# Two query blocks moved from beside the scan into the opening of a hybrid decoder layer

## The chip, the cores and the metric

The kernel runs on one core of a Trainium2 chip. The metric is the device time of one execution, in microseconds (us), as the median of several runs. The engines are named as in the profile: PE (TensorE, matrix products; PEld is its weight load), DVE (VectorE), ACT (ScalarE), POOL (GpSimd) and SP (SyncE, which here only issues transfers). Each has its own queue and works through it in order; semaphores join them. PE writes its results to PSUM, eight banks of 512 f32 values a partition, from which DVE or ACT copies them out.

## What is computed

One layer of a decoder, for a prompt of 1024 tokens and 8 single sample tokens that share the weights (1032 columns of tokens in all). All of it is in f32. With `xn` the root-mean-square norm of `x`:

```
sc_b, sc_c, sc_x, z, xbc, dt_raw, q, gates = split(xn @ w_in)      # w_in: 1024 x 12320
y_a = (sc_b * conv3(sc_c * sc_x)) @ w_sc_out
xs, B, C = split(silu(conv4(xbc) + bias));  dt = softplus(dt_raw + dt_bias)
y_b = group_rmsnorm((ssd(xs, dt, a, B, C) + d * xs) * silu(z)) @ w_ssm_out
y_c = softmax(q . k_mem / 16) . v_mem @ w_attn_o                   # 4 heads of 256, 256 memory tokens
x  += (g_a * y_a + g_b * y_b + g_c * y_c) @ w_merge_o
x  += swiglu(rmsnorm(x));   y = rmsnorm(x)
```

`ssd` is a state-space scan over 8 chunks of 128 tokens, in 4 groups of 8 heads. The columns of `w_in` that matter here are `xbc` (24 blocks of 128 columns; block 16 is B of group 0, called B0, and block 20 is C of group 0, called C0), `dt_raw` (32 columns), and `q` (8 blocks of 128, two to a head).

## The kernel before

Every projection is computed in blocks of 128 output columns for all 1032 tokens. A weight block of 1024 x 128 is loaded raw (512 KB, `load_raw`, line 139, one of three buffers), then split into a rounded part `hi` (an ACT cast) and the rest `lo` (a DVE subtraction). The activations are split likewise into `ah` and `al`. A product is then three passes, hi x ah, hi x al and lo x ah, over 8 pieces of the 1024 inputs. In `gemm` (line 218) the 1032 tokens are taken as 260 + 512 + 260 columns, so a block is 8 x 3 x 3 = 72 matmuls into three PSUM banks.

The stages that matter here are these.

The opening makes xn. The tokens are taken in four quarters of 256 (the last has 264, with the sample tokens). For a quarter, `square` sums squares (ACT), `root_of` makes the inverse root on ACT and DVE, turns it by PE (`ps_rb`, line 516) and copies it to `rbc`. `tokens` then turns two of the eight 128-wide pieces at a time by PE (`ps_xt`), scales them on DVE (`xw`, line 522), casts on ACT (`xnh`, line 523), subtracts on DVE (`xnl`, line 524), and copies the turned x to a buffer `xt` and stores it. Beside this, `first_products` (lines 597 to 599) computes B0 and C0 for the quarter before, 3 matmuls of 256 columns for each piece and block, and `step_sizes` (line 607) computes `dt_raw` with 16 small matmuls a quarter. B0 and C0 have three PSUM banks each (`ps_b0`, `ps_c0`); two more are shared by all the turns (`sm_ps`). After the opening comes the turn of the step sizes (`ps_dtT`, line 692) and the first two blocks of z (`z_step`).

Then follow long stages for z, xbc, the gates and the short convolution, which the change doesn't touch.

The scan stage comes after the last gate pair. Its work is cut into small pieces, which stand in a queue `pend`. Matrix blocks, called fillers, run on PE in between: 8 query blocks (`q_step`, which projects one block, scales it on ACT, copies the sample columns to `qs` and stores the block to `q_d`), then blocks of the output projections (`out_part`, `wo0x`, `wo1x`, `wo2x`). `pace` says how many pieces are issued in each block: the length of `pend` over 18 blocks (8 fillers, 8 of the first output projection and 2 of the second). The attention then is cut up in the same way, beside the output blocks that are left, less 1.4 (14 - 1.4 = 12.6 blocks).

The order of instructions on each engine is set by a scheduler that works from the program's order and its own estimates, and not by the program text alone.

Of the kernel before, what the change touches and what calls it, by code (L numbers as in the profile page):

```python
# [43 lines left out]
def tile_kernel(ctx: ExitStack, tc, a, o):  # L44
# [3 lines left out]
    def f32(t):  # L48
        return t.bitcast(F32)
# [390 lines left out]
    with tc.tile_pool(name="p0", bufs=1) as p0, tc.tile_pool(name="pop", bufs=1, space=PSUM) as pop:  # L440
        ps_b0, ps_c0 = (
            [pop.tile([P, 512], F32, tag=f"{n}{i}", name=f"ps_{n}{i}") for i in range(3)] for n in ("B", "C")
        )
        xin = []
# [8 lines left out]
        for col, name in ((16 * P, "wB0"), (20 * P, "wC0")):  # L453
            loaded[name] = load_raw(wblock(w_in, C_XBC + col), name)
        w_dt = load_raw(wblock(w_in, C_DT), "wdt")
        for i in range(2, NCK):
            load_x(i)
        xs_sb = p0.tile([NS, D], F32, tag="xs", name="xs_sb")
        SY.dma_start(xs_sb, a["x_sample"][:, 0, :])

        PC["mix"] = 200
# [9 lines left out]
        for key, src, n in (  # L471
# [13 lines left out]
            while done < n:  # L485
                b, off = divmod(at, P)
                m = min(n - done, P - off)
                SY.dma_start(rows[off : off + m, b, :], r[done : done + m, :])
                done += m
                at += m  # L490
        def par(key, i):
            return prm[:, PC[key] + i : PC[key] + i + 1]
# [65 lines left out]
        def root_of(g):  # L558
# [3 lines left out]

            ps = sm_ps(f"ps_rb{g}") if g else ps_c0[2]
            turn(g, ps, 0, lambda i, t, n: bc(rst[:n, 2 * g + i : 2 * g + i + 1], [n, P]))
# [24 lines left out]

        def first_products(g, k):  # L590
            c, n = part(g), parts[g][1]
            ah, al = xn[k]
            ks = slice(k * P, (k + 1) * P)
            for ps, (wh, wl) in ((ps_b0, w_b0), (ps_c0, w_c0)):
                bank, at_c = places[g]
                po = ps[bank][:, at_c : at_c + n]
                PE.matmul(po, wh[:, ks], ah[:, c], start=(k == 0), stop=False)
                PE.matmul(po, wh[:, ks], al[:, c], start=False, stop=False)
                PE.matmul(po, wl[:, ks], ah[:, c], start=False, stop=(k == order[-1]))

        def step_sizes(g):
# [3 lines left out]
            for k in range(KD):  # L605
                q = k % 4
                PE.matmul(
                    ps[q * HEADS : (q + 1) * HEADS, :n], w_dt[:, k * P : k * P + HEADS], xw[k][:, c],
                    start=(k < 4), stop=(k >= 4),
# [8 lines left out]
        with tc.issue_after(mix_in):  # L618
            square(0, 1)
        ahead_ = [sm_ps(f"ps_xt0{i}") for i in range(2)] + [ps_b0[1], ps_c0[1]]  # L620
        for i, (t, n) in enumerate(srcs[0]):
# [4 lines left out]
        for g in range(4):  # L626
            steps_ = [order[2 * i : 2 * i + 2] for i in range(4)] if g < 3 else [(k,) for k in order]
            for i, ks in enumerate(steps_):
                last_x, scaled = tokens(g, ks)
                if g == 0 and i == 0:  # L630
                    w_b0, w_c0 = first_weights(scaled, last_x)
# [12 lines left out]
        firsts = [ev_tile("u" + n) for n in ("B0", "C0")]  # L644
        for u, ps in zip(firsts, (ps_b0, ps_c0)):
            S.copy(u[:, 3 : 3 + 512], ps[0])
            S.copy(u[:, 3 + 512 : 3 + 768], ps[1][:, :256])
        for k in order[:4]:
            first_products(3, k)
        step_sizes(3)  # L650
        for k in order[4:]:
            first_products(3, k)
        for u, ps in zip(firsts, (ps_b0, ps_c0)):
            S.copy(u[:, 3 + 768 : 3 + TT], ps[2][:, : TT - 768])

# [768 lines left out]
    def plain():  # L1424
        loaded["wq0"] = load_raw(wblock(w_in, C_Q), "wq0")
        load_group(0)
# [13 lines left out]
    fillers = deque()  # L1440
    for i in range(8):
        fillers.extend(q_step(i))
# [76 lines left out]
    for g in range(GROUPS):  # L1519
# [747 lines left out]
```

## Time and profile before

| | us |
|---|---|
| median of 3 runs | 2427.4 (2425.25 to 2427.65) |
| profiled execution | 2428.33 |
| its span | 2426.6 |
| PE busy in the span | 2397.0 |
| DVE busy | 1613.8 |
| ACT busy | 1091.9 |

The profile is one execution, recorded instruction by instruction. A row of the timeline has the start, the duration, the engine, the line of the kernel, the operation, and out<-in by the names of the tiles, with the shape and a count. Where the engine was idle before it, square brackets say how long, and whose result ended the wait. Successive matmuls overlap in the pipeline, so their durations add up to more than the time they take; the distance from start to start tells the pace. A row of a table of stretches has the stretch, its length, the busy time and the number of instructions of PE, PEld, DVE, ACT and POOL, the granted PE clock, the share of time in which the transfer engines were busy, and GB/s. A row of the waits has the total, the number and the longest.

### The profile page before, as it was taken

The numbers are of one execution on the slowest core, as the hardware profiler recorded it, in microseconds if no ns is written. First come the engines' busy times: TensorE is split into PE (matmuls) and PEld (weight loads), VectorE is DVE, ScalarE is ACT, GpSimd is POOL, SyncE is SP. The second block draws the span as 40 slices with busy tenths as digits, with TensorE's granted clock in tenths as the row PEclk, the third lists the DMA queues.
The fourth block names the chain that finished last, engine by engine and source line by source line (L and its number), as shares of the span: only waits on it lengthen the run. The fifth ranks groups of instructions, "written<-read, shape, count | busy, mean of one in ns | idle before, by whom it ended". The sixth has DMA issues, their size and how long they took to land. (4 is left out here: it accounts for less than half of the span.)

```text
span 2426.6 us, 45180 instructions
## 1 busy us (share of the span) xinstructions
PE 2397.0 (99%) x18716; PEld 2279.9 (94%) x18716; DVE 1613.8 (67%) x2597; ACT 1091.9 (45%) x1740; POOL 106.9 (4%) x163
## 2 busy tenths in 40 slices
PE   8999999999999999999999999999999999999998
PEld 6999999999999999888888887899999999999998
DVE  6844677777777675568687773454777655567965
ACT  6643555455453543656555542223543333343423
POOL 0000000000000000212212000000000000000000
PEclk9999999999999999999999999999999999999999
DMA  6444423444354345768887797864455333354622
GB/s 203 136 150 164 135 84 114 140 140 131 112 158 118 106 126 179 225 223 272 257 283 215 252 337 234 276 213 150 148 178 168 101 104 103 94 178 154 192 88 79
DMA packets 357716, 407.94 MB, mean 168 GB/s; under 512 B 16270, under 2 KB 277502, under 8 KB 357503
## 3 DMA queue, kind: packets, MB, share of 16 engines
q1 hardware_dynamic: 334374, 341.79, 45.2%
q10 hardware_dynamic: 23137, 63.26, 6.8%
q8 instruction: 147, 2.41, 0.4%
q14 instruction: 58, 0.48, 0.1%
HBM read 288.85 MB, written 116.38 MB: 167 GB/s over the span
## 5 line engine op out<-in xcount | busy, mean ns | idle before, releaser
L1007 ACT ACTIVATE r<-r,acum 128x128 f32<-128x128 f32 x256 | 79.3, 391 | 3.5 <-DMA r<-ac_d 2.6
L796 DVE SCALAR_TENSOR_TENSOR ax<-u,prm,ax 128x1024 f32<-128x1024 f32 x44 | 56.4, 1282 | 0.0
L948 ACT ACTIVATE st<-st,es 128x128 f32<-128x128 f32 x128 | 41.3, 392 | 19.1 <-DMA st<-in_state_ssm_dram 14.5
L1040 POOL TENSOR_TENSOR xdd<-xdt,decst 128x512 f32<-128x512 f32 x32 | 34.3, 1072 | 284.2 <-DVE xdt L1036 278.4
L1034 DVE TENSOR_TENSOR r<-r,cbm 128x1024 f32<-128x1024 f32 x32 | 39.2, 1224 | 4.3 <-ACT r L1009 2.4
L950 DVE SCALAR_TENSOR_TENSOR st<-sr,dts,st 128x128 f32<-128x128 f32 x128 | 41.0, 355 | 0.4
L1059 DVE TENSOR_TENSOR y<-po,ea 128x512 f32<-128x512 f32 x28 | 19.3, 690 | 31.3 <-PE po L1055 31.3
L1076 PE MATMUL pss<-xdd,bT 128*128 128x512 f32 x64 | 34.5, 620 | 3.7 <-ACT bT L1033 3.1
L954 DVE SCALAR_TENSOR_TENSOR sr<-st,sr 128x128 f32<-128x128 f32 x128 | 36.1, 292 | 1.1
L1497 DVE TENSOR_TENSOR yr<-po,yr 128x1032 f32<-128x1032 f32 x8 | 9.8, 1230 | 39.5 <-PE po L218 39.5
L1063 PE MATMUL py<-r,xdt 128*64 128x128 f32 x512 | 35.0, 279 | 0.0
L1009 ACT ACTIVATE r<-r 128x1024 f32<-128x1024 f32 x32 | 33.9, 1058 | 0.7
L1089 POOL TENSOR_TENSOR s<-s,cdec 128x512 f32<-128x512 f32 x28 | 33.1, 1181 | 1.8 <-DVE s L1082 1.5
L1883 DVE TENSOR_TENSOR x<-pm,xT 128x516 f32<-128x516 f32 x15 | 10.4, 694 | 32.3 <-PE pm L1869 32.3
L1800 DVE TENSOR_TENSOR gt<-po,gt 128x1032 f32<-128x1032 f32 x8 | 9.9, 1232 | 32.4 <-PE po L218 31.1
L1063 PEld LDWEIGHTS py<-r,xdt 128*64 128x64 f32 x512 | 27.3, 136 | 4.4 <-issue 1.0
L1055 PE MATMUL po<-bc,s 128*128 128x128 f32 x224 | 29.6, 275 | 0.0
L1055 PEld LDWEIGHTS po<-bc,s 128*128 128x128 f32 x224 | 28.0, 191 | 1.0
L1612 ACT ACTIVATE pr<-psa,mx 128x256 f32<-128x256 f32 x32 | 14.9, 470 | 30.1 <-DVE mx L1610 30.1
L799 DVE SCALAR_TENSOR_TENSOR ax<-u,prm,ax 128x1032 f32<-128x1032 f32 x22 | 28.4, 1290 | 0.0
L1600 DVE SCALAR_TENSOR_TENSOR kc<-kc,qb 128x256 f32<-128x256 f32 x64 | 23.9, 423 | 6.3 <-DMA qb<-qs_d 6.3
L793 ACT ACTIVATE ax<-u,prm 128x1024 f32<-128x1024 f32 x22 | 27.4, 1246 | 1.2 <-ACT u L875 0.4
(9245 smaller groups left out, 8948.9 us busy)
## 6 DMA issues: line engine op xcount, KB each, us to landing
r<-ac_d SPq DMA_DIRECT2D x32, 512.0 KB
gt_d<-G ACTq DMA_DIRECT2D x24, 516.0 KB
gt<-gt_d SPq DMA_DIRECT2D x24, 516.0 KB
xs_d<-ax ACTq DMA_DIRECT2D x22, 516.0 KB
zs<-zs_d SPq DMA_DIRECT2D x16, 516.0 KB
yb_d<-x SPq DMA_DIRECT2D x16, 516.0 KB
in<-yb_d SPq DMA_DIRECT2D x16, 516.0 KB
st<-in_state_ssm_dram SPq DMA_DIRECT2D x32, 256.0 KB
```

Source lines behind the costliest of these rows:

```text
L796: V.scalar_tensor_tensor(acc[:, :T], u[:, j : j + T], w[j], acc[:, :T], op0=ALU.mult, op1=ALU.add)
L948: S.activation(st[:, i], st[:, i], AF.Copy, scale=es[:, g * 4 + i, b : b + 1])
L950: V.scalar_tensor_tensor(st[:, i], rb, dts[:, g * 4 + i, b : b + 1], st[:, i], op0=ALU.mult, op1=ALU.add)
L954: V.scalar_tensor_tensor(rb, st[:, i], 1.0, rc, op0=ALU.mult, op1=ALU.mult, accum_out=ys[:, g * 4 + i, b : b + 1],)
L1007: S.activation(r[:, j, :], r[:, j, :], AF.Relu, scale=-1.0, bias=acum[:, c, h : h + 1])
L1009: S.activation(r, r, AF.Exp, scale=-1.0)
L1034: V.tensor_tensor(r, r, bc(cbm.unsqueeze(1), [P, HPG, P]), op=ALU.mult)
L1040: G.tensor_tensor(b3(xdd, HPG), b3(xdt, HPG), bc(decst[:, c, hs].unsqueeze(2), [P, HPG, 64]), op=ALU.mult)
L1055: PE.matmul(po[:, t * P : (t + 1) * P], state["s"][:, t * P : (t + 1) * P], bcg[1][:, cs], start=True, stop=True,)
L1063: PE.matmul(py[hp : hp + 64, (h // 2) * P : (h // 2 + 1) * P], xdt[:, h * 64 : (h + 1) * 64], r[:, (h % 2) * 4 + h // 2, :], start=True, s ...
L1076: PE.matmul(pss, bT, xdd, start=True, stop=True)
L1089: G.tensor_tensor(b3(s_new, HPG), b3(state["s"], HPG), bc(cdec[:, c, hs].unsqueeze(2), [P, HPG, 64]), op=ALU.mult,)
```

## The change

Query blocks 0 and 1 are computed in the opening, by quarters of the tokens, beside B0 and C0. In the third quarter's loop PE gets the query products of the first quarter, in the fourth quarter's those of the second; the products of the third and fourth quarters follow the loop. B0 and C0 for the third quarter are put into the fourth quarter's loop as before, one after the other since they share a bank.

The four blocks share six PSUM banks, `pb`. A bank holds a block's first two quarters, is copied out, and is used again for the last one; the third quarters have half a bank each in two further banks. `first_out` copies from there into the output tiles, in three parts.

The step-size weights are loaded as 32 columns (128 KB) instead of 128 (512 KB), into a buffer of their own and behind the x tiles. The two raw query blocks are loaded after the rows of parameters, and z's first two weight blocks after them. The buffers `xt` become three instead of four.

Beside the scan 6 query blocks are left. The pieces of the scan are spread over 17 blocks (6 + 8 + 3), those of the attention over 13 - 1.4 = 11.6. The turn of the step sizes, which stood in `pend`, is called in its place.

```diff
-        ps_b0, ps_c0 = (
-            [pop.tile([P, 512], F32, tag=f"{n}{i}", name=f"ps_{n}{i}") for i in range(3)] for n in ("B", "C")
-        )
+        pb = [pop.tile([P, 512], F32, tag=f"o{i}", name=f"ps_o{i}") for i in range(6)]
...
-        w_dt = load_raw(wblock(w_in, C_DT), "wdt")
         for i in range(2, NCK):
             load_x(i)
         xs_sb = p0.tile([NS, D], F32, tag="xs", name="xs_sb")
         SY.dma_start(xs_sb, a["x_sample"][:, 0, :])
+        w_dt = p0.tile([P, KD, HEADS], F32, tag="wdt", name="wdtr")
+        SY.dma_start(w_dt, w_in[:, C_DT : C_DT + HEADS].rearrange("(k p) c -> p k c", p=P))
...
+        q_raw = [load_raw(wblock(w_in, C_Q + i * P), f"wq{i}") for i in range(2)]
...
-        places = ((0, 0), (0, 256), (1, 0), (2, 0))
+        places = {
+            "B": ((0, 0), (0, 256), (2, 0), (0, 0)),
+            "C": ((1, 0), (1, 256), (2, 256), (1, 0)),
+            "q0": ((3, 0), (3, 256), (5, 0), (3, 0)),
+            "q1": ((4, 0), (4, 256), (5, 256), (4, 0)),
+        }
...
-            xt = p0.tile([P, 512], F32, tag="xt", bufs=4, name=f"xt{g}{ks[0]}")
+            xt = p0.tile([P, 512], F32, tag="xt", bufs=3, name=f"xt{g}{ks[0]}")
...
+        def query_weights():
+            wts["q0"] = [wp.tile([P, 1024], F32R, tag=t, name=f"wq0{t}") for t in ("whi", "wlo")]
+            wts["q1"] = [p0.tile([P, 1024], F32R, tag=t, name=f"wq1{t}") for t in ("qhi", "qlo")]
+            for n, raw in zip(("q0", "q1"), q_raw):
+                hi, lo = wts[n]
+                S.copy(hi, raw)
+                V.tensor_sub(lo, raw, f32(hi))
...
+        def first_out(n, g0):
+            t, u = (outs_[n][:, 3:], outs_[n]) if n in "BC" else (outs_[n], None)
+            lo = parts[g0][0]
+            w = 512 if g0 == 0 else parts[g0][1]
+            bank, at_c = places[n][g0]
+            src = pb[bank][:, at_c : at_c + w]
+            if u is not None:
+                S.copy(t[:, lo : lo + w], src)
+            else:
+                S.activation(t[:, lo : lo + w], src, AF.Copy, scale=QS)
...
-                if g:
-                    for k in ks:
-                        first_products(g - 1, k)
+                if g == 1:
+                    first_products("BC", 0, ks)
+                    if i == 2:
+                        query_weights()
+                elif g == 2:
+                    first_products("BC", 1, ks)
+                    first_products(("q0", "q1"), 0, ks)
+                elif g == 3:
+                    first_products("BC"[i // 4], 2, order[i % 4 * 2 : i % 4 * 2 + 2])
+                    first_products(("q0", "q1"), 1, ks)
...
+            if g == 2:
+                for n in "BC":
+                    outs_[n] = ev_tile("u" + n + "0")
+                    first_out(n, 0)
+        for n in ("q0", "q1"):
+            outs_[n] = ev_tile(n)
+            first_out(n, 0)
+        for i in range(2):
+            loaded[f"wz{i}"] = load_raw(wblock(w_in, C_Z + i * P), f"wz{i}")
+        for n in ("q0", "q1"):
+            first_products((n,), 2, order)
+        for n in "BC":
+            first_out(n, 2)
+        first_products("BC", 3, order[:4])
         step_sizes(3)
-        for k in order[4:]:
-            first_products(3, k)
+        first_products("BC", 3, order[4:])
+        for n in ("q0", "q1"):
+            first_out(n, 2)
+        for n in "BC":
+            first_out(n, 3)
+        first_products(("q0", "q1"), 3, order)
+        for i, n in enumerate(("q0", "q1")):
+            first_out(n, 3)
+            G.tensor_copy(qs[:, i, :], outs_[n][:, T:TT])
+            SY.dma_start(q_d[i], outs_[n][:, :TT])
...
-    pend.extend([dt_turn, lambda: history("state_ssm_conv", h_xc, 16, ev_tile("hist", (24, D)))])
+    dt_turn()
+    pend.extend([None, lambda: history("state_ssm_conv", h_xc, 16, ev_tile("hist", (24, D)))])
...
-        loaded["wq0"] = load_raw(wblock(w_in, C_Q), "wq0")
+        loaded["wq2"] = load_raw(wblock(w_in, C_Q + 2 * P), "wq2")
...
-    for i in range(8):
+    for i in range(2, 8):
         fillers.extend(q_step(i))
...
-    pace[:] = len(pend) / (len(fillers) + KD + 2) + 1e-6, 0.0
+    pace[:] = len(pend) / (len(fillers) + KD + 3) + 1e-6, 0.0
```

More of the change, by code (lines that the diff above doesn't have):

```diff
@@ L504, in tile_kernel @@
         parts = [(g * 256, 256 if g < 3 else 264) for g in range(4)]
-        places = ((0, 0), (0, 256), (1, 0), (2, 0))
+        places = {
[4 rows of a table added]
+        }
+        wts = {}
         srcs = [[(t, P) for t in xin[2 * g : 2 * g + 2]] for g in range(4)]
@@ L561, in root_of @@
             ins = rsqrt(p0, rst[:, cs], st[:, cs], D, [P, m], f"x{m}")
-            ps = sm_ps(f"ps_rb{g}") if g else ps_c0[2]
+            ps = sm_ps(f"ps_rb{g}") if g else pb[2]
             turn(g, ps, 0, lambda i, t, n: bc(rst[:n, 2 * g + i : 2 * g + i + 1], [n, P]))
@@ L588, in first_weights, with first_product, first_products @@
                 yield hi, lo
-        def first_products(g, k):
-            c, n = part(g), parts[g][1]
+        def first_product(n, g, k):
+            c = part(g)
             ah, al = xn[k]
+            wh, wl = wts[n]
             ks = slice(k * P, (k + 1) * P)
[L594 to L599, printed above, removed]
+            bank, at_c = places[n][g]
+            po = pb[bank][:, at_c : at_c + parts[g][1]]
+            PE.matmul(po, wh[:, ks], ah[:, c], start=(k == 0), stop=False)
+            PE.matmul(po, wh[:, ks], al[:, c], start=False, stop=False)
+            PE.matmul(po, wl[:, ks], ah[:, c], start=False, stop=(k == order[-1]))
+        def first_products(names, g, ks):
+            for k in ks:
+                for n in names:
+                    first_product(n, g, k)
+        def query_weights():
[5 more added lines that the diff above has]
+                V.tensor_sub(lo, raw, f32(hi))
+        outs_ = {}
+        def first_out(n, g0):
[8 more added lines that the diff above has]
+                S.activation(t[:, lo : lo + w], src, AF.Copy, scale=QS)
         def step_sizes(g):
@@ L607, in step_sizes @@
                 PE.matmul(
-                    ps[q * HEADS : (q + 1) * HEADS, :n], w_dt[:, k * P : k * P + HEADS], xw[k][:, c],
+                    ps[q * HEADS : (q + 1) * HEADS, :n], w_dt[:, k, :], xw[k][:, c],
                     start=(k < 4), stop=(k >= 4),
@@ L619, in tile_kernel @@
             square(0, 1)
-        ahead_ = [sm_ps(f"ps_xt0{i}") for i in range(2)] + [ps_b0[1], ps_c0[1]]
+        ahead_ = [sm_ps(f"ps_xt0{i}") for i in range(2)] + pb[4:]
         for i, (t, n) in enumerate(srcs[0]):
@@ L630, in tile_kernel @@
                 if g == 0 and i == 0:
-                    w_b0, w_c0 = first_weights(scaled, last_x)
+                    wts["B"], wts["C"] = first_weights(scaled, last_x)
                 if g == 2 and i == 0:
@@ L643, in tile_kernel @@
                 step_sizes(g - 1)
[L644 to L648, printed above, removed]
-            first_products(3, k)
-        step_sizes(3)
-        for k in order[4:]:
-            first_products(3, k)
-        for u, ps in zip(firsts, (ps_b0, ps_c0)):
-            S.copy(u[:, 3 + 768 : 3 + TT], ps[2][:, : TT - 768])
+            if g == 2:
[12 more added lines that the diff above has]
+        first_products("BC", 3, order[:4])
+        step_sizes(3)
+        first_products("BC", 3, order[4:])
[8 more added lines that the diff above has]
+            SY.dma_start(q_d[i], outs_[n][:, :TT])
+        firsts = [outs_[n] for n in "BC"]
         SY.dma_start(r_d, rbc[0:1, :])
```

## The prediction

> **What bounds the kernel now.** I read the page's shares and slices first, then a table of stretches that I cut at the stages the change touches, then the rows of the opening in order of time, then the waits.
>
> ```profile
> span 2426.6 us, 45180 instructions
> PE 2397.0 (99%) x18716; PEld 2279.9 (94%) x18716; DVE 1613.8 (67%) x2597; ACT 1091.9 (45%) x1740; POOL 106.9 (4%) x163
> PE   8999999999999999999999999999999999999998
> ```
>
> TensorE (PE) is busy in every slice but the first and last. So moving work pays only where PE now has holes, and costs wherever it makes new ones. The stretches (PE busy, then PEld, DVE, ACT, POOL, granted clock, DMA share, GB/s):
>
> ```profile
> 0.00:28.70 28.70, 20.79 (x117) 17.78 (x118) 17.92 (x58) 18.40 (x40) 1.04 (x8) 1.00 0.88 282
> 28.70:60.78 32.08, 30.53 (x243) 24.08 (x242) 21.70 (x53) 21.41 (x52) 0.57 (x3) 0.95 0.42 132
> 60.78:84.00 23.22, 23.22 (x153) 20.93 (x152) 20.58 (x38) 15.69 (x25) 0.00 (x0) 1.00 0.47 148
> 980.00:1132.70 152.70, 151.34 (x1094) 128.18 (x1093) 99.78 (x125) 91.04 (x189) 37.52 (x37) 1.00 0.70 227
> 1132.70:1333.20 200.50, 196.90 (x1366) 166.24 (x1364) 157.98 (x184) 110.72 (x214) 33.52 (x31) 1.00 0.80 256
> 1333.20:1472.80 139.60, 135.34 (x885) 121.11 (x885) 93.24 (x251) 66.36 (x135) 0.00 (x0) 1.00 0.80 280
> 1472.80:1565.00 92.20, 89.53 (x623) 74.36 (x622) 34.85 (x42) 23.75 (x45) 0.00 (x0) 1.00 0.77 257
> ```
>
> Rows one and two are the opening, up to the first z product; three is the two z blocks; four and five the scan with its q and first output blocks; six and seven the attention with the rest. In the last four PE is idle for 1.36 + 3.60 + 4.26 + 2.67 = 11.9 us of 585. The second row says 30.53 of 32.08 busy, but a matmul's row lasts longer than its share of the pipeline, so the real hole there comes from start-to-start spacings:
>
> ```profile
> 24.26 0.28 PE L597 MATMUL ps_B<-xnh,wB0h 128*128 128x256 f32 x1
> 24.97 0.28 PE L597 MATMUL ps_B<-xnh,wB0h 128*128 128x256 f32 x1
> ...
> 28.70 0.40 PE L516 MATMUL ps_rb<-ident,rst 128*128 128x128 f32 x2
> 28.94 0.60 PE L516 MATMUL ps_xt<-ident,x 128*128 128x128 f32 x4
> 29.62 1.07 PE L607 MATMUL ps_dt<-xw,wdtr 128*32 128x256 f32 x16
> 30.62 0.39 PE L597 MATMUL ps_B<-xnh,wB0h 128*128 128x256 f32 x1
> 30.85 0.27 PE L597 MATMUL ps_C<-xnh,wC0h 128*128 128x256 f32 x1
> ...
> 31.71 0.60 PE L516 MATMUL ps_xt<-ident,x 128*128 128x128 f32 x4
> 32.14 0.38 PE L573 MATMUL ps_prm<-ident,rows 128*128 128x128 f32 x2
> ...
> 48.74 0.42 PE L598 MATMUL ps_C<-xnl,wC0h 128*128 128x264 f32 x1
> 48.96 0.42 PE L599 MATMUL ps_C<-xnh,wl 128*128 128x264 f32 x1
> ...
> 58.83 1.87 PE L692 MATMUL ps_dtT<-fold,dtr 128*128 128x32 f32 x16
> 60.78 0.74 PE L218 MATMUL ps_z<-xnh,wz0h 128*128 128x260 f32 x3
> ...
> 62.30 0.64 PE L218 MATMUL ps_z<-xnh,wz0h 128*128 128x260 f32 x3
> 65.12 0.63 PE L218 MATMUL ps_z<-xnh,wz0h 128*128 128x260 f32 x3
> ```
>
> Six quarter products lie between 24.26 and 24.97: 0.12 us each. Sixteen step-size rows take 1.00 us (29.62 to 30.62), four transposes 0.43 us (31.71 to 32.14), the turn of the step sizes 1.95 us (58.83 to 60.78), and the first product after other work about 0.1 us more than its neighbours (30.62 to 30.85 is 0.23). How many products fall on either side of 28.70 (line 597 alone, one product in three):
>
> ```profile
> 0.00:28.70 28.70, 8.19 (x28) 5.78 (x28) 1.00 0.88 282
> 28.70:60.78 32.08, 10.04 (x36) 6.41 (x36) 0.95 0.42 132
> ```
>
> So from 28.70 to 60.78 PE had 36 x 3 x 0.12 = 13.0 us of products, 44 transposes of tokens x 0.11 = 4.8, roots and parameters 0.6, step sizes 4 x 1.0 = 4.0, their turn 1.95, and some 20 switches x 0.1 = 2.0: 26.4 us of 32.08. The hole to be filled there is 5.7 us. It includes the spell around 48.8 where products follow at 0.22 us, nearly twice the usual spacing.
>
> **The change part by part.** *Removed:* two q blocks beside the scan, 72 matmuls each. z0 has the same shapes: six groups of three from 62.30 to 65.12 is 0.47 us a group, so 24 groups are 11.3 us and two blocks 22.6 us of PE on the path.
>
> *Added:* the same two blocks as 2 x 4 quarters x 8 x 3 = 192 quarter products of 0.12 us: 23.0 us of PE, all after 28.70, since the query weights are converted only near the end of the second quarter. 18 or so are placed between that point and the third quarter's root, where PE waited; the last 19 us of the opening's PE order (144 products x 0.12 and 2 us of step sizes) depend on little but weights and xn already made. If PE has no other idle time, the opening gets longer by 23.0 - 5.7 = 17.3 us. Bounds: 16.6 (with what the earlier x gives, below) and 25.1 (nothing filled, and the 2.1 us of casts in the way). I take a value near the lower one, because between 28.70 and the end the new order always has some product ready in front of a wait.
>
> *The query weights on ACT and DVE:* two casts and two subtractions, placed before the square root for the third quarter. The nearest rows are those of z0's weights:
>
> ```profile
> 27.56 0.21 ACT L106 ACTIVATE rs_t<-rs_v 128x2 f32<-128x2 f32 x1
> 30.10 0.80 ACT L523 CAST xnh<-xw 128x256 fp32r<-128x256 f32 x2 [2.33 <-DVE xw L522]
> 40.76 0.20 ACT L106 ACTIVATE rs_t<-rs_v 128x3 f32<-128x3 f32 x1
> 42.33 1.05 ACT L167 CAST wz0h<-wz0r 128x1024 fp32r<-128x1024 f32 x1
> 44.43 1.22 DVE L168 TENSOR_TENSOR wz0l<-wz0r,wz0h 128x1024 fp32r<-128x1024 f32 x1
> 12.91 1.06 ACT L556 ACTIVATE junk<-x 128x1024 f32<-128x1024 f32 x1 [0.68 <-DMA x<-in_x_prompt_dram]
> ```
>
> That puts the root at 27.56 off by 2.1 us on ACT; behind it wait, in turn, four small DVE steps, PE's ps_rb, the copy to rbc and the casts that now start at 30.10, about 3 us late in all. What covers it is the query products: their first needs only the first cast, at 28.6. From the third quarter's root PE has 14 us of work to the fourth's (92 products, 16 transposes, one set of step sizes), while ACT needs 10.7 us (30.10 to 40.76) from its first cast to its own part of that root, so ACT catches up and PE sets the pace. I charge 0.6 us for the start. Without that cover it is the 2.1 us.
>
> *Loads:* the step-size weights shrink from 512 KB to 128 KB and move behind the x tiles; two raw q loads of 512 KB enter SP's queue where the bias load stood.
>
> ```profile
> 2.81 2.96 SPq L139 DMA_DIRECT2D wdtr<-in_w_in_dram  x1
> 20.82 0.36 SPq L496 DMA_DIRECT2D bias<-in_ssm_dt_bias_dram  x1
> 22.84 0.40 SPq L139 DMA_DIRECT2D wz0r<-in_w_in_dram  x1
> ```
>
> The x tiles behind wdtr come up to 1 us earlier; ACT waited 0.68 us for one at 12.91, so this is worth 0 to 0.7 and I take 0.4. The q loads are issued at about 20 to 22 and read at 27.6 and 28.6, with some 6 us to land. If they take longer, ACT stands still with the root, casts and copies behind it, and each microsecond late delays the third quarter by one. z0 and z1 weights move behind them but are read only near the end.
>
> *Third token buffer, six banks shared, outputs:* three xt buffers instead of four can make ACT wait for a store in the last quarter; the 19 us of ready products cover it. The banks' second use waits for ACT copies that stand ahead of the products in its order, and B and C halves of one bank follow one another; nothing. The q copies (under 0.6 us each) end just before z0, which waits only for its weight cast, earlier in ACT's order. The two q stores go to SP ahead of the second memory tile and the history, under 1 us later, with z0's own products as cover. The z stretch is tight on DVE (20.58 of 23.22), but wz1's subtraction leaves it and wz0's comes earlier: nothing, at worst 1 us.
>
> *17 blocks beside the scan for 18, and 11.6 for 12.6 beside the attention:* the same scan and attention pieces at 6 to 9% closer steps. The waits named now:
>
> ```profile
> PE pss L1076 <- ACT bT L1033: 3.1, 5, 1.5
> PE pso L1650 <- DMA vc<-in_cache_mem_v_dram: 1.2, 1, 1.2
> ```
>
> They and their like are some 15 waits of at most 1.5 us. A step of about 2.2 us gets 0.13 us shorter, so they grow by 1 to 2 us; the bounds are 0 and 11.3 (one block's time not won at all). I take 1.5, near the small end, because 11.9 of 585 us is the whole idle time there.
>
> Sum: -22.6 + 17.3 + 0.6 - 0.4 + 1.5 = -3.6 us. The profiled execution took 2428.3 us around its span of 2426.6, 0.9 above the median of 2427.4; taken from the median this gives 2423.8. A change of 0.2% is 4.9 us, about what a measurement of this kernel can tell from none.
>
> The slow spell at 48.74 bears on the filling: the granted clock of that stretch is 0.95, so cold products cost about 0.05 x 32.08 = 1.6 us of the 5.7. The Trainium skill, "TensorE: Matmul & The Clock Gate", Part 1, says that the clock is gated to half by default and after an idle window of some 3.4 us, and released by sustained activity. By that rule the spell goes once PE is dense, which agrees with the spacing of 0.22 against 0.12 and leaves the sum as it is; were the spell to stay, it would be 1.6 us worse, -2.0.
>
> **The rivals.** *More is won (2421.0):* the loads land early, the start costs nothing, the scan's waits don't grow: -22.6 + 16.6 = -6.0, and a little of the old idle beside the two q blocks goes too. For it: PE idles only 0.9% of stretch four. Against: stretch five, with DVE at 79%, has more waits, and eleven of its kind of blocks now carry the scan.
>
> *The holes are latency and stay (2429.9):* the opening grows by 23.0 + 2.1, the change wins nothing: +2.5. For it: the third quarter begins on a chain ACT, DVE, PE, DVE, ACT. Against: the added products stand in that chain's gaps.
>
> *The attention doesn't shrink (2433.6):* stretch six moves data 0.80 of the time, and its keys, values and q tiles are the same bytes in one block less: 0.80 x 139.6 / 128.3 = 0.87. If loads then end last, one block's 11.3 us is not won and the 1.5 falls into it: -5.1 + 11.3 = +6.2. It decides from the point where PE's idle time in stretches four to seven grows from 11.9 to above about 17, and is a loss beyond 0.2% from 22. For it: a wait for vc is already there. Against: it is 1.2 us, once.
>
> **How the numbers follow.** My forecast 0.45 (own range 2421.5 to 2427), more won 0.20, latency stays 0.15, attention held 0.20. Faster by over 0.2% is below 2422.5: the second case and a third of the first, 0.35. Slower is above 2432.3: the last case and a little of the third, 0.22. The rest, 0.43, is within. The range 2419.5 to 2433.0 leaves out half the last case and a small part of the second.
>
> **What would show it.** In the changed profile: the first z product at 77.5 to 79.5 us (60.78 now); PE without named waits over 1 us after 30 us; quarter products at 0.12 us through the fourth quarter; the scan and attention stretch, from the first q product to the last wo2 product, about 21 us shorter, with 12 to 15 us of PE idle in it. Wrong would be: ACT waiting for wq0r near 27, z0 after 82, or PE waits for DMA or DVE in the attention that add up to 5 us more.

## The result and the profile after

The changed kernel takes 2439.9 us (median of 4 runs, 2437.5 to 2442.0) against 2427.1 us (4 runs): the ratio is 1.0054, with a 95% interval of 1.0036 to 1.0071. It is 0.5% slower, 16 us above the forecast of 2423.8, and above the upper end of the prediction's range, 2433.0.

The page of the changed kernel, shares and PE's slices:

```profile
span 2439.9 us, 45265 instructions
PE 2401.2 (98%) x18764; PEld 2285.4 (94%) x18764; DVE 1615.5 (66%) x2597; ACT 1092.2 (45%) x1744; POOL 114.8 (5%) x163
PE   8999999999999999999999989999999999999998
```

There is an 8 in slice 24 now, which covers 1403 to 1464 us and lies in the attention. But PE is also busy for 4.2 us longer than before, for the same mathematics (2397.0). So one must look by stage. The stretches of the changed kernel (columns as before: PE, PEld, DVE, ACT, POOL, clock, DMA share, GB/s), cut at the same instructions as those of before:

```profile
0.00:28.70 28.70, 21.01 (x119) 18.24 (x119) 17.70 (x55) 19.77 (x41) 1.04 (x8) 0.88 0.91 292
28.70:79.50 50.80, 50.06 (x431) 45.28 (x431) 26.02 (x60) 25.28 (x61) 2.04 (x5) 1.00 0.36 107
79.50:104.30 24.80, 24.59 (x162) 22.00 (x160) 19.04 (x37) 15.89 (x26) 0.21 (x1) 1.00 0.44 149
1003.30:1332.70 329.40, 321.30 (x2277) 270.58 (x2278) 251.34 (x299) 193.17 (x394) 77.35 (x66) 0.99 0.76 249
1332.70:1562.20 229.50, 219.77 (x1464) 190.44 (x1463) 124.10 (x292) 88.06 (x177) 0.00 (x0) 0.99 0.78 264
```

The clock of 0.88 in the first row is a spell at half clock from 11 to 18 us; the openings of E1 and E9 below have none there and take 79.2 us, so it cost at most 0.3 us. Rows four and five are the scan (first q product to the fourth block of the second output projection, wo13) and the attention (wo13 to the first block of the merge, wo30). In the profile of before these two cuts are:

```profile
980.40:1327.20 346.80, 341.98 (x2422) 290.12 (x2423) 254.74 (x302) 198.46 (x399) 71.03 (x68) 1.00 0.77 245
1327.20:1552.50 225.30, 218.58 (x1463) 188.80 (x1463) 120.74 (x288) 86.40 (x176) 0.00 (x0) 1.00 0.77 265
```

The whole span, from the starts of these marks, with four of the runs below (E1 new opening alone, E2 scan alone, E9 and E12 the gate's product taken off DVE, in the changed kernel and in the one before):

| us | before | after | E1 | E2 | E9 | E12 |
|---|---|---|---|---|---|---|
| opening, to the first z product | 60.8 | 79.5 | 79.2 | 59.4 | 79.2 | 59.5 |
| from there to the scan | 919.6 | 923.8 | 923.1 | 920.6 | 922.1 | 919.8 |
| scan | 346.8 | 329.4 | 346.3 | 329.9 | 323.7 | 351.9 |
| attention | 225.3 | 229.5 | 223.0 | 227.2 | 227.6 | 219.0 |
| scan and attention | 572.1 | 558.9 | 569.3 | 557.1 | 551.3 | 570.9 |
| from the attention to the end | 874.1 | 877.7 | 876.3 | 875.0 | 877.3 | 875.3 |

After against before: +18.7, +4.2, -13.2 and +3.6, which gives the 13.3 us between the spans. The forecast had +17.5 for the opening, -21.1 for scan and attention and nothing for the rest.

The opening came out near the forecast. Rows of the changed kernel's PE in order of time:

```profile
28.40 0.28 PE L605 MATMUL ps_o<-xnl,wq0whi 128*128 128x256 f32 x1
29.44 0.39 PE L606 MATMUL ps_o<-xnh,wq0wlo 128*128 128x256 f32 x1 [0.76 <-DVE wq0wlo L619]
...
73.55 0.28 PE L604 MATMUL ps_o<-xnh,wq1qhi 128*128 128x264 f32 x1
73.67 0.28 PE L605 MATMUL ps_o<-xnl,wq1qhi 128*128 128x264 f32 x1
...
79.51 0.74 PE L218 MATMUL ps_z<-xnh,wz0h 128*128 128x260 f32 x3
```

PE waits once, for 0.76 us, for the first q block's low part; after that there is no named wait up to z0, the products follow at 0.12 us, and z0 stands at 79.5.

The shortfall is beside the scan and the attention. PE's waits there in the changed kernel, scan first, then attention (total, number, longest):

```profile
PE po L218 <- DVE b01l L178: 1.4, 1, 1.4
PE py L1118 <- DVE xdt L1091: 1.1, 1, 1.1
PE xp L1084 <- DVE y L1233: 0.9, 1, 0.9
PE po L218 <- DVE b00l L178: 0.9, 1, 0.9
PE po L1110 <- DVE s L1134: 0.9, 1, 0.9
...
PE psa L1750 <- DVE wo23l L168: 2.8, 1, 2.8
PE psv L1782 <- ACT ot L1785: 2.1, 1, 2.1
PE psp L1764 <- ACT pr L1668: 1.4, 1, 1.4
```

Before, the scan's waits were mostly for ACT's `bT` and a load; now DVE ends seven of the ten that the view names there. By the stretches, PE's idle time grew from 4.82 + 6.72 = 11.5 us to 8.10 + 9.73 = 17.8. The busy time fell by 19.5 us instead of 22.6. The missing 3.1 us is about what two spells at half clock account for, one at 1264 to 1271 us and one at 1448 to 1456, of 1.7 us each (time by one less the granted clock).

The place is the seam at which the second output projection begins. Rows of the changed kernel in order of time there, PE:

```profile
1264.93 0.73 PE L218 MATMUL po<-b00h,wo10h 128*128 128x260 f32 x3 [0.58 <-ACT b00h L177]
1266.57 0.75 PE L218 MATMUL po<-b00l,wo10h 128*128 128x260 f32 x3 [0.91 <-DVE b00l L178]
...
1272.53 0.74 PE L218 MATMUL po<-b01l,wo10h 128*128 128x260 f32 x3 [1.35 <-DVE b01l L178]
...
1276.01 1.16 PE L1110 MATMUL po<-bc,s 128*128 128x128 f32 x8 [0.85 <-DVE s L1134]
```

and DVE:

```profile
1265.29 1.23 DVE L178 TENSOR_TENSOR b00l<-in,b00h 128x1032 fp32r<-128x1032 f32 x1
1266.43 4.90 DVE L1255 SCALAR_TENSOR_TENSOR x<-x,prm,sqa 128x1032 f32<-128x1032 f32 x4
1271.25 1.23 DVE L178 TENSOR_TENSOR b01l<-in,b01h 128x1032 fp32r<-128x1032 f32 x1
```

The four scalings of a group norm (L1255, 4.9 us in a row) stand on DVE between the first two splits that PE needs. In the kernel before they are over first:

```profile
1246.96 4.91 DVE L1200 SCALAR_TENSOR_TENSOR x<-x,prm,sqa 128x1032 f32<-128x1032 f32 x4
...
1254.14 1.23 DVE L178 TENSOR_TENSOR b00l<-in,b00h 128x1032 fp32r<-128x1032 f32 x1
1255.28 1.23 DVE L178 TENSOR_TENSOR b01l<-in,b01h 128x1032 fp32r<-128x1032 f32 x1
```

There b01l is ready 8 us before the block that reads it begins, at 1264.4. The stretch of the seam in the changed kernel:

```profile
1264.00:1288.00 24.00, 20.05 (x122) 15.63 (x122) 23.65 (x27) 17.84 (x34) 5.48 (x4) 0.93 0.86 302
```

DVE is busy for 23.65 of 24.00 us, and PE for 20.05. DVE's share over the whole scan is only 76% (251.34 of 329.40); here it has no room left. ACT, busy for 17.84 us, ends one of the four waits above, DVE three.

### The profile page after: what moved, and what is told of

Same layout as the page of the kernel before. It is cut to its first block, busy times and chain, and to the rows that moved or that the text cites. A ratio compares the mean times of both kernels' runs of the same rounds, so it can differ in the third digit from the quotient of the medians.

```text
span 2439.9 us, 45265 instructions
## 1 busy us (share of the span) xinstructions
PE 2401.2 (98%) x18764; PEld 2285.4 (94%) x18764; DVE 1615.5 (66%) x2597; ACT 1092.2 (45%) x1744; POOL 114.8 (5%) x163
## 4 chain that ended last, share of the span: by engine, by line
PE 87%; DVE 5%; DMA 4%; ACT 2%; issue 1%; SPq 0%; DVEq 0%; ACTq 0%
PE po L218 11%; PE pm L1925 4%; PE ps_q L218 2%; PE py L1118 1%; PE po L1110 1%; PE pss L1131 1%; PE ps_z L218 1%; PE X17m L267 1%; PE G16m L267 1%; PE d00m L267 1%; PE G22m L267 1%; PE Z14m L267 1%; PE Z10m L267 1%; PE Z6m L267 1%; PE Z8m L267 1%
## 5 line engine op out<-in xcount | busy, mean ns | idle before, releaser
L1114 DVE TENSOR_TENSOR y<-po,ea 128x512 f32<-128x512 f32 x28 | 19.3, 689 | 26.4 <-PE po L1110 26.1
L1088 ACT COPY bT<-bp 128x128 f32<-128x128 f32 x32 | 8.4, 262 | 45.8 <-DVE cbm L1086 45.8
```

## The experiments

Theory 1, as it stood after the first look: the opening costs about what it should, and the fewer blocks save less than they hold because DVE and the pieces are late where they stand closest. Rivals: the loss is in the opening or in the stages behind it; and closeness is not the reason.

**E1, the new opening alone** (q0 and q1 are computed in the opening and again beside the scan):

```diff
-    for i in range(2, 8):
+    for i in range(8):
...
-    pace[:] = len(pend) / (len(fillers) + KD + 3) + 1e-6, 0.0
+    pace[:] = len(pend) / (len(fillers) + KD + 2) + 1e-6, 0.0
```

> The changed opening alone: query blocks 0 and 1 are computed in the opening, and computed once more beside the scan, with 8 fillers and 18 blocks as in the kernel before. Theory 1 (the loss lies in the scan and the attention, whose pieces now stand closer): the opening costs its 18.7 us and nothing else changes, so 18 to 20 us over the kernel before, with the stretch from the first z product to the scan as long as before. Theory 2 (the new opening also makes the later, untouched stages slower, which in the profile of the changed kernel were 4.2 us longer up to the scan and 3.6 us longer after the attention): 25 to 27 us over the kernel before.

Measured: 2449.6 against 2426.5 us, ratio 1.0095 (1.0080 to 1.0110), +23.1: between the two. Its opening is 79.2 us. Of the rest, 3.5 us come between z0 and the scan.

**E2, the scan alone** (the old opening; six fillers and the changed pace; blocks 0 and 1 are left out and blocks 2 and 3 stored in their place too):

```diff
-    for i in range(8):
+    for i in range(2, 8):
...
-    pace[:] = len(pend) / (len(fillers) + KD + 2) + 1e-6, 0.0
+    pace[:] = len(pend) / (len(fillers) + KD + 3) + 1e-6, 0.0
```

> The other half alone: the opening of the kernel before, 6 fillers, 17 blocks beside the scan. Query blocks 0 and 1 are left out; blocks 2 and 3 are stored a second time in their place, so that loads and stores of the attention are as many. The prediction's step (22.6 us of PE less, 1.5 us of new waits): 21 us under the kernel before. Theory 1: the scan gets 17.4 us shorter and the attention 4.1 us longer as in the changed kernel, so 13 us under the kernel before. Theory 2: about 21 us under it, since the opening is the old one.

Measured: 2417.2 us, ratio 0.9966 (0.9954 to 0.9979): -9.3 of the 22.6 us taken away. 23.1 - 9.3 = +13.8: the parts add up to the change's 12.8, so neither disturbs the other much. The profile is the fastest of the six runs (2413.8), so its stages flatter it by some 3 us. The old opening takes 59.4 us here, 1.4 less than in the profile of before. Two of E2's waits, with the same names as in the changed kernel:

```profile
PE po L218 <- DVE b01l L178: 2.8, 1, 2.8
...
PE po L218 <- DVE b00l L178: 0.9, 1, 0.9
```

So the seam's wait comes with the missing blocks, not with the opening.

**E3 and E4, the pace** (the pieces of the scan over 18 blocks, and over 16; 6 + 8 + 4 and 6 + 8 + 2):

```diff
-    pace[:] = len(pend) / (len(fillers) + KD + 3) + 1e-6, 0.0
+    pace[:] = len(pend) / (len(fillers) + KD + 4) + 1e-6, 0.0     # E3; E4: KD + 2
```

> The changed kernel with the scan's pieces over 18 blocks instead of 17, so 10.6 blocks are left for the attention instead of 11.6. Theory 1: the scan has the step of the kernel before again and loses about 3 us of its PE idle time, the attention gets 2 to 4 us more; in sum within 3 us of the changed kernel. Theory 2 (the waits of these stages matter little): the same time as the changed kernel to 1 us.

> The changed kernel with the scan's pieces over 16 blocks, which leaves the attention 12.6 blocks as in the kernel before. Theory 1: the scan's idle time grows by 3 to 5 us, the attention's falls back by 4 us; within 3 us of the changed kernel. Theory 2: the same time as the changed kernel to 1 us.

Measured: E3 2444.2 (1.0067, 1.0052 to 1.0082), E4 2436.5 us (1.0041, 1.0026 to 1.0056), both against 2426.5. Looser pieces are no better: E3's scan and attention take 565.9 us. E4's scan is 333.7 us and its attention 224.9: together 558.6, as in the changed kernel. In E3 the first two splits are done before the norm begins (b01l at 1258.1, the norm at 1270.3), and PE has no wait for either. E4's norm is done before the first split, as in the kernel before, but waits for a load, DVE and ACT take the place:

```profile
PE xp L1084 <- DMA x<-xs_d: 3.3, 3, 1.4
PE po L1110 <- DVE s L1134: 3.2, 2, 2.2
PE po L218 <- ACT b00h L177: 2.2, 2, 1.6
```

So it is not one unlucky order alone.

**E5, one block** (q0 alone in the opening; seven fillers, the pieces over 17 blocks and the attention over 12.6):

```diff
-            for n, raw in zip(("q0", "q1"), q_raw):
+            for n, raw in zip(("q0",), q_raw):
...
-    for i in range(2, 8):
+    for i in range(1, 8):
...
-    pace[:] = len(pend) / (len(fillers) + KD + 3) + 1e-6, 0.0
+    pace[:] = len(pend) / (len(fillers) + KD + 2) + 1e-6, 0.0
```

> Only query block 0 goes into the opening (96 quarter products instead of 192); 7 fillers, the scan over 17 blocks, the attention over 12.6 blocks as in the kernel before. Theory 1 (the opening has about 4 to 5 us of holes to fill, and what else is put in costs its full length; the attention loses only where it is pressed into fewer blocks): z starts 11.5 - 4.5 = 7 us later, the scan gets 7 to 11 us shorter, the attention stays; 0 to 4 us under the kernel before, or as far over it if the later stages lose 3 to 4 us as they did with two blocks. Theory 3 (each block taken from beside the scan gives only half its time, whatever is done): 1 to 3 us over the kernel before.

Measured: 2432.6 (10 runs) against 2426.5 us (19), ratio 1.0020 (1.0010 to 1.0029). The stretches of its scan and attention:

```profile
993.70:1330.20 336.50, 330.30 (x2350) 279.85 (x2351) 255.84 (x301) 195.73 (x397) 78.79 (x67) 1.00 0.76 249
1330.20:1551.90 221.70, 218.38 (x1465) 188.98 (x1464) 120.71 (x288) 86.73 (x175) 0.00 (x0) 1.00 0.77 270
```

One block less gives 572.1 - 558.2 = 13.9 us, as much as two give in the changed kernel, at a clock of 1.00 and with 6.2 + 3.3 us of idle PE. By these profiles the second block is worth nothing. E5's opening takes 68.0 us and the stages from z0 to the scan 6.1 us more than before, so E5 loses outside.

**E6, the attention closer, nothing else** (the kernel before, its attention over 11.6 blocks):

```diff
-        pace[:] = len(pend) / (len(outs) - 1.4) + 1e-6, 0.0
+        pace[:] = len(pend) / (len(outs) - 2.4) + 1e-6, 0.0
```

> The kernel before with one edit: the attention's pieces over 11.6 blocks instead of 12.6. Opening and scan are as before. Theory 1 (an attention closer by one block makes PE wait, and a long enough wait also halves the clock for a while): the attention gets 3 to 5 us longer, with a stretch of lower granted clock, so 3 to 5 us over the kernel before. The prediction's step (waits hardly grow): within 1 us of it.

Measured: 2430.3 (10 runs) against 2426.5 us (19), ratio 1.0010 (0.9999 to 1.0021). The attention takes 226.65 us against 225.3, at full clock: 1.3 us of the 4.2 by which it grew. The median is 3.8 us up, as theory 1 said, but the interval includes no change, and the profile has neither the longer attention nor the spell that theory 1 asks for: scan and attention together take 571.2 us, 0.9 less than before. E6 settles neither side. Its opening has the second look at the old one (a stretch and the first z product):

```profile
28.70:59.40 30.70, 29.14 (x243) 23.05 (x241) 21.58 (x53) 21.40 (x52) 0.57 (x3) 1.00 0.43 137
...
59.44 0.74 PE L218 MATMUL ps_z<-xnh,wz0h 128*128 128x260 f32 x3
```

**E7, splits on POOL** (eight of the output projections' subtractions before and in the seam):

```diff
-        V.tensor_sub(lo, src, f32(hi))
+        (G if on_pool[0] else V).tensor_sub(lo, src, f32(hi))
...
+        on_pool[0] = (i, m) in ((0, KD - 1), (1, 0))
```

> The changed kernel with eight subtractions, those that split the inputs of the second output projection, on POOL instead of DVE. In the changed kernel PE waited there for DVE (b00l, b01l, s) and its clock fell. Theory 1 (DVE is the late engine at that seam, since the scan's norm and the split fall together): these waits and the low clock there go, 2 to 5 us under the changed kernel. Rival (the data itself is late, or POOL is slower still): the waits only change their name, 0 to 5 us over the changed kernel.

Measured: 2442.7 against 2426.5 us, ratio 1.0073 (1.0050 to 1.0096). The waits only take another name:

```profile
PE po L1112 <- DVE s L1139: 2.5, 3, 1.0
PE po L220 <- POOL b00l L180: 2.0, 1, 2.0
PE po L1112 <- DVE s L1136: 1.5, 1, 1.5
```

This speaks for the rival, or for POOL being too slow at it. The rows of POOL and DVE at the seam show the latter, and more:

```profile
1262.66 2.65 POOL L180 TENSOR_TENSOR b00l<-in,b00h 128x1032 fp32r<-128x1032 f32 x1 [3.21 <-ACT b00h L179]
...
1263.12 9.04 DVE L1257 SCALAR_TENSOR_TENSOR x<-x,prm,sqa 128x1032 f32<-128x1032 f32 x4
```

A split takes 2.65 us here where DVE needs 1.2, and DVE's four scalings, which run beside two such splits, take 9.04 us instead of 4.9. So E7 didn't relieve DVE at the seam and tests theory 1 only badly; E9 does it without POOL.

**E8, four tiny loads more** behind the opening, to shift which semaphores the later transfers use:

```diff
+        lane = p0.tile([8, 4], F32, tag="lane", name="lane")
+        for i in range(4):
+            SY.dma_start(lane[:, i : i + 1], a["x_sample"][:, 0, i : i + 1])
```

> The changed kernel with four more tiny loads at the end of the opening, so that the count of transfers, and with it the semaphore each later transfer uses and waits for, is that of the kernel before again (it was shifted by four). Theory 4 (the shifted semaphores make later transfers land late, as X10r did, 3.4 us of waiting on DVE instead of 1.9): the wait of G8m and the longer d stretch go, 2 to 4 us under the changed kernel. If they stay, the semaphores are not the cause: the same time to 1 us.

Measured: 2440.9 us, ratio 1.0056 (1.0040 to 1.0072). A wait of 1.1 us for G8m, which for the changed kernel is shown further down, stays, so the semaphores are not its cause. (This profile's opening takes 83.7 us, with a second spell at half clock from 28 to 35 us, and z0 to the scan 921.3.)

**E9, the gate's product off DVE** (eight products beside the scan are made plain copies on ACT; the gate's product is left out):

```diff
-            V.tensor_mul(gt[:, :TT], flat(ps), gt[:, :TT])
+            S.copy(gt[:, :TT], flat(ps))
```

> The changed kernel, with the eight products with the gate after the first output projection replaced by plain copies on ACT (the gate's product is left out), which takes some 8 x 1.1 us from DVE beside the scan. Theory 1: DVE is late with the splits of the second output projection's inputs at the seam at 1264 to 1286 us, because the same pieces now stand closer, so with DVE freed the waits of PE for b00l, b01l, xdt and s there go, the half-clock spell at 1264 us with them, and from the first q product to wo13 it takes 325.5 to 327 us (329.4 in the changed kernel): 2436 to 2438 us in all. Rival (the pieces themselves are chains of several engines that the fewer blocks no longer cover; whichever engine is relieved, another name ends the wait): 328.5 to 330 us, the waits renamed, the spell still there, 2439 to 2442 us.

Measured: 2433.2 against 2427.5 us, ratio 1.0028 (1.0015 to 1.0042): +5.7, where the changed kernel has +12.8. Its scan and attention, and DVE at the seam:

```profile
1001.30:1325.00 323.70, 318.78 (x2278) 269.68 (x2278) 241.23 (x290) 201.16 (x402) 76.31 (x66) 1.00 0.78 253
1325.00:1552.60 227.60, 219.43 (x1465) 190.61 (x1464) 124.29 (x292) 87.64 (x177) 0.00 (x0) 0.99 0.78 268
...
1250.94 1.22 DVE L178 TENSOR_TENSOR b00l<-in,b00h 128x1032 fp32r<-128x1032 f32 x1
...
1259.25 4.89 DVE L1255 SCALAR_TENSOR_TENSOR x<-x,prm,sqa 128x1032 f32<-128x1032 f32 x4
1264.06 1.22 DVE L178 TENSOR_TENSOR b01l<-in,b01h 128x1032 fp32r<-128x1032 f32 x1
```

10 us of DVE gone (251.3 to 241.2), and the scan is 5.7 us shorter, more than theory 1 said. PE's waits for b00l and b01l are gone, and so is the half-clock spell beside the scan. The order on DVE isn't that of the changed kernel, though: the norm still stands between the first two splits, but the first is issued 8 us ahead of it, and all three are over before PE reads b01l at 1265.85. So E9 changes DVE's load and its order together.

**E10 and E11, the slots.** The new opening takes two evacuation buffers more and shifts the weight buffers by one, so all later tiles lie at other addresses. E10 is the changed kernel with unused tiles taken, so that the slots are those of before; E11 is the kernel before with the slots of the changed one. No instruction differs.

```diff
+    for i in range(3):            # E11: 2
+        ev_tile(f"turn{i}")
+    for i in range(2):            # E11: 1
+        for t in ("raw", "whi", "wlo"):
+            wp.tile([P, 1024], F32, tag=t, name=f"turn_{t}{i}")
```

> The changed kernel, with tiles that nothing uses taken behind the opening, three of the five-slot evacuation buffers and two of the three-slot weight buffers, so that from z0 on each tile has the slot that it had in the kernel before. No instruction is added or moved. Theory 1: the 4.2 us that z0 to the scan has grown come from other addresses of the same tiles, so z0 to the scan goes back from 923.8 to some 919.6 us, PE's waits for G8m (1.1 us) go, and the time is 2435 to 2437 us. Rival (transfers that land a little later against the same engines' order, whatever the slots): G8m's wait stays, z0 to the scan 922 to 924 us, 2439 to 2442 us.

> The kernel before, with tiles that nothing uses taken behind the opening, two of the evacuation buffers and one of the weight buffers, so that from z0 on each tile has the slot that it has in the changed kernel. No instruction is added or moved. Theory 1 (slots): z0 to the scan grows from 919.6 to some 923.8 us with waits of PE for G8m as in the changed kernel, 2430 to 2432 us. Rival (not the slots): 919 to 921 us, no wait for G8m, 2426 to 2428 us.

Measured: E10 2443.5 (1.0069, 1.0054 to 1.0084), E11 2428.8 us (1.0007, 0.9998 to 1.0016), against 2427.5. From z0 to the scan E10 takes 923.9 us and E11 920.3: not the slots. But E11's attention takes 228.5 us with the same instructions as before, against 225.3, with a wait of 4.0 us for `ot` and a half-clock spell.

**E12, the control to E9** (the same edit in the kernel before):

```diff
-            V.tensor_mul(gt[:, :TT], flat(ps), gt[:, :TT])
+            S.copy(gt[:, :TT], flat(ps))
```

> The kernel before, with the same eight products with the gate replaced by copies on ACT (the gate's product is left out): the control to the run of the changed kernel with that edit, which took 5.7 us off its scan. Theory 1 (DVE is the bound only where 17 blocks carry the scan and the seam falls on its busiest stretch): with 18 blocks DVE has room, from the first q product to wo13 it stays at 345 to 347 us (346.8 without the edit), 2425 to 2428 us in all. Rival (less DVE work helps the scan in any case, and the closer pieces have no part in it): 340 to 342 us, 2420 to 2422 us.

Measured: 2426.9 (10 runs) against 2429.4 us (13), ratio 0.9994 (0.9983 to 1.0004): no difference that can be told. Its stretches:

```profile
979.30:1331.20 351.90, 346.17 (x2444) 292.60 (x2445) 248.37 (x298) 209.10 (x411) 73.11 (x68) 1.00 0.76 245
1331.20:1550.20 219.00, 214.11 (x1442) 186.30 (x1441) 119.38 (x284) 82.37 (x171) 0.00 (x0) 1.00 0.79 268
```

22 matmuls have moved over the cut between the two (2444 for 2422), so only the sum can be compared: 570.9 against 572.1 us, -1.2. The same relief gave the changed kernel 558.9 - 551.3 = 7.6. How far one profile can be trusted for this, the other runs tell: the sum is 569.3 to 573.7 us in the profiles with eight fillers (before, E1, E6, E11) and 557.1 to 560.9 in those with six and the changed pace on DVE as it was (after, E2, E8, E10). E12 lies among its own, E9 lies 5.8 us below the lowest of its own. By medians the two are less far apart: E9 is 12.8 - 5.7 = 7.1 us nearer to the kernel before than the changed kernel is, and E12 is 2.5 us below it, with no change inside its interval. The two blocks are worth 570.9 - 551.3 = 19.6 us when DVE is eased in both, and 13.2 us when it isn't.

## Why the prediction was wrong

*The step that failed* is the last of the sum: "A step of about 2.2 us gets 0.13 us shorter, so they grow by 1 to 2 us; the bounds are 0 and 11.3. I take 1.5." The two stages shrank by 13.2 of the 22.6 us taken out, so it measured 9.4 us, near the upper end (5.2 beside the scan, 4.2 beside the attention). The value was taken from a mean: idle time over a stage, and a step shortened by 6 to 9%. What the runs show in its place is DVE: with 10 us less on it (E9) the changed kernel regains 7.6 us of these stages, and the kernel before (E12) only 1.2.

The rows show where it falls. The second output projection begins behind 16 of the 18 blocks in the kernel before, so with 89% of the pieces issued, and behind 14 of 17, 82%, in the changed one. The seam's eight splits (1.2 us each) now meet a group norm that still has its 4.9 us of scalings to do, and for 24 us DVE has no room. In E5 (15 of 17, 88%) these waits are absent and one block gives 13.9 us. That this phase is the reason is argued, not shown: E3 (14 of 18) and E4 (14 of 16) don't have the norm between the splits and gain nothing by it, since the pieces wait elsewhere, and E9 changed DVE's order too. E7's failure is the fault of the replacement: a wait for POOL's b00l of 2.0 us in place of DVE's 0.9, and scalings that took 9.04 us for 4.9.

4.2 of the 9.4 us lie in the attention, by which it grew with as many matmuls as before (1464 for 1463). A half-clock spell holds 1.7 of them. E6's attention, closer by a block, is 1.3 us longer, and E11's, with the same instructions as before, 3.2. So the rest can't be put down to the change from single profiles.

Of the 16.9 us between the forecast's -3.6 and the spans' +13.3, this step is 7.9; 7.8 are stages that were priced at nothing, and 1.2 the opening.

*The opening* was priced at +17.5 and grew by 18.7; z0 came at 79.5, at the upper edge of 77.5 to 79.5. But its "hole of 5.7 us" was partly an accident of the one execution that I read. The spell around 48.8 us, which the sum let the new products fill, is not in E6's opening: granted 1.00 there and z0 at 59.4, as in E2, E11 and E12 (59.4 to 59.5). Against these the opening grew by 20 us, and the hole was 30.7 - 26.4 = 4.3. That part of the loss was in the trace as a clock of 0.95, and I should have taken the 1.6 us out of the hole. The Trainium skill, "TensorE: Matmul & The Clock Gate", Part 1, has the clock released by sustained activity: the changed kernel's stretch from 28.70 to 79.50 has 1.00, which agrees, but the spell wasn't the old opening's own.

*ACT and loads.* The casts waited for no load, and PE lost 0.76 us to the first q block's low part, against 0.6 charged for the start. Right.

*The stages "which the change doesn't touch"* were priced at nothing and grew by 4.2 us ahead of the scan and 3.6 behind the attention. From z0 to the scan the four further profiles with the old opening take 919.8 to 920.6 us, the eight with the two-block opening 921.3 to 923.9. When the starts of the same PE products are compared, the changed kernel loses its 4.2 us at four places: 1.2 us between 116 and 127 us, 1.5 in a half-clock spell at 318 to 322, 1.2 at 699 and 0.3 at 999.5. The spell is in some of the profiles only. The third place is in all eight (waits of 0.7 to 1.2 us) and in none with the old opening. The changed kernel's wait, what DVE waited for just before, and the same DVE row in the kernel before:

```profile
PE G8m L267 <- DVE G L381: 1.0, 1, 1.0
...
693.36 0.69 DVE L352 TENSOR_TENSOR X10sa<-X10r 128x512 f32<-128x512 f32 x1 [3.40 <-DMA X10r<-in_w_in_dram]
...
670.37 0.69 DVE L352 TENSOR_TENSOR X10sa<-X10r 128x512 f32<-128x512 f32 x1 [1.85 <-DMA X10r<-in_w_in_dram]
```

DVE waits for the load of X10r for 3.1 to 4.1 us in the eight profiles and for 1.9 to 2.0 in the five with the old opening, and its work for PE is late by that. Semaphores (E8) and slots (E10, E11) are excluded as the reason, and behind the z blocks PE, DVE and ACT have the same order of instructions in both kernels, but for the names of the query blocks. Why the load lands later stays open. Behind the attention the further profiles with the old opening take 875.0 to 876.4 us and those with the new one 875.3 to 877.7, so most of the 3.6 us is that the one profile of before had 874.1.

*The rivals.* "The attention doesn't shrink" named nearly the right size, 11.3 us not won where 9.4 were, and its sign, idle time above about 17 us, was met (17.8). But the place and the reason were others: 5.2 us of it are beside the scan, and in the attention PE waited for loads for 0.9 us (1.2 before), while its largest waits were for DVE and ACT. "More is won" named stretch five, with DVE at 79%, as what spoke against it; the seam lies there, and the forecast quoted that figure and didn't price it. "The holes are latency" had the opening at +25.1; it grew by 18.7, or 20.1 against the openings without the spell.

Even with DVE eased the change doesn't pay: E9 against E12 is +19.7 for the opening, +2.3 up to the scan, -19.6 and +2.0 to the end, which is the 4.4 us between their spans (6.4 between their medians). The products of the two blocks take about as much PE time in the opening (23.0 us by the prediction's rows) as beside the scan (22.6), and the opening gave back only 3 to 4 us of it (23.0 less 20.1 or 18.7).

## What to carry to other kernels

Blocks that run between pieces of other work are cover as well as cost. Before taking some away, look at the busiest 20 or 30 us of the second engine and not at its share of the stage, and at which piece meets which block when the pace shifts. And count a hole only if a second profile has it too: a half-clock spell in one execution is no room.

## What was not expected of the hardware

The half-clock spells last 3.4 us or twice that, and cost 1.7 or 3.4 us of PE time (time by one less the granted clock; E4, with 0.66 granted from 1269 to 1279 us, and E7, with 0.66 from 1264 to 1274, have the longer kind). No profile with eight fillers has one beside the scan, nor has E5's; of those with six all but E9's have, in the changed kernel behind PE waits that add up to only 1.5 us (0.58 + 0.91 up to 1266.6, with the product groups 0.7 us apart from 1267 on, for 0.47). One stands in the gate stage, in the changed kernel but not in the one before:

```profile
316.00:320.00 4.00, 4.00 (x33) 3.78 (x33) 2.70 (x9) 0.89 (x2) 0.17 (x3) 0.81 0.18 75
320.00:324.00 4.00, 4.00 (x29) 4.00 (x29) 2.13 (x5) 1.80 (x3) 0.00 (x0) 0.77 0.81 250
```

PE's rows fill it (4.00 of 4.00 us), and still the granted clock falls to 0.81 and 0.77. The same Part 1 of the Trainium skill puts the halving behind an idle window of about 3.4 us, and names a kernel in which frequent short idles between groups of products brought it about. The spell at the seam followed 1.5 us of waits, which fits the second better than the first; the one at 318 us followed no idle time that the rows show, which fits neither, and there the measurement decides. Small transposes of 8 x 8 stand just before that spell. They stand in the kernel before as well (293 to 298 us), without a spell, so they alone don't bring it.

In E7 four scalings took 9.04 us on DVE instead of 4.9 while POOL ran two splits beside them: the first two took 3.3 and 3.4 us, the two behind POOL's work 1.3 each.
